# One core of Trainium2: where the context's two SSD chunks get their gate, and how often a rotary table is loaded

## The chip, the cores and the metric

The kernel runs on one core of one Trainium2 chip. The time is that of one execution on the device, in microseconds (us). Engines are called as the profile calls them: PE is TensorE's matmuls and transposes, PEld its weight loads, DVE is VectorE, ACT ScalarE, POOL GpSimd, and SP the engine whose queue issues nearly all DMAs.

## The reference, cut to what matters

The model has one even layer (a bidirectional Mamba-2 SSD group beside windowed attention) and one odd layer (S5 with GLU). The stream is 256 context tokens and 2048 latent tokens, 18 chunks or tiles of 128 tokens in all; chunks 0 and 1 are the context. The two places of the change are `ssd_output`, which every chunk passes once, and `apply_rope`, which only latent tiles pass.

```python
def ssd_output(y, xs, z, d_skip, norm_w):
    bsz, L = y.shape[:2]
    y = (y + xs * d_skip[:, None]).reshape(bsz, L, SSD_INNER)
    return rmsnorm(y * jax.nn.silu(z), norm_w)

def apply_rope(t, cos, sin):
    half = t.shape[-1] // 2
    t1, t2 = t[..., :half], t[..., half:]
    ...
    return jnp.concatenate([t1 * cos - t2 * sin, t1 * sin + t2 * cos], axis=-1)

def even_layer(x, xc, c, c_ctx, ...):
    proj = norm_mod(x, norm_w, shift, scale) @ w_in
    proj_c = norm_mod(xc, norm_w, shift_c, scale_c) @ w_in
    z, xbc, dt_raw, q, kv, g = jnp.split(proj, EVEN_SPLITS, axis=-1)
    ...
    y_c, h_f, h_b = ssd_bidir(xs_c, bm_c, cm_c, dt_c, a, h0, h0)
    y, _, _ = ssd_bidir(xs, bm, cm, dt, a, h_f, h_b)
    ssd_out = ssd_output(y, xs, z, d_skip, ssd_norm_w)
    ...
    q = apply_rope(q.reshape(bsz, L, ATT_HEADS, ATT_HEAD_DIM), cos, sin)
    k = apply_rope(k, cos, sin)
    att = window_attention(q, k, v, k_c, v_c, sink) * jax.nn.silu(g)
    x = x + gate * (jnp.concatenate([ssd_out, att], axis=-1) @ w_out)
    if ctx_out:
        ssd_c = ssd_output(y_c, xs_c, z_c, d_skip, ssd_norm_w)
        ...
```

The odd layer and the final norm come behind this and are not touched.

## The kernel before, in words

**Stages.** After some 165 us of conditioning come the input projection with the SSD sweeps (to about 1508 us in the profiled execution), attention with half of the even layer's output projection woven in (to about 2330 us), and the rest: the other half of the output projection and the odd layer.

**Matrix products.** A projection is made of three matmuls for each piece (`mm3`, lines 312 to 314: high by high, low by high, high by low parts). On PE these are the rows `mm<-xTh,wh`, `mm<-xTl,wh` and `mm<-xTh,wl` (operands the other way round in blocks that make features).

**The order of the work.** PE's order is written by hand: `even_in` makes two generators, `stream1` (the projection's blocks) and `stream2` (the SSD sweep), and `merge` (line 813) lets `stream2` have a turn whenever it has earned the PE time that a `yield` names. The other engines' orders are worked out by a scheduler from dependencies. Each engine then runs its own list strictly in order, and an instruction that waits holds all behind it on its engine; SP's DMA issues stand in such a list too.

**The backward sweep.** `stream2` first does the forward sweep, then the backward sweep `ssd_ba(c)` (line 1011) over chunks 1, 0, 17, 16, ..., 2. In `ssd_ba` PE does, for each half g, `off` (line 951) and `st` (line 928), the state's update with the tiles `xw` and `bt`. The part behind it is:

```python
        self.ssd_gt()
        if c < 2:
            nc.sync.dma_start(self.yp_d[tk, :], y)
        else:
            self.ssd_gate(c, y)
```

So the gate of chunk c is begun at the end of `ssd_ba(c)`, and its transposes (`ssd_gt`) stand one chunk later. Chunks 0 and 1 only store y there, since their z columns are projected last; their gates follow at the end of `stream2`, with y loaded back.

**The gate.** `ssd_gate` (line 1037) loads z from DRAM on SP (line 1045) and then goes from engine to engine: POOL z*y (1046), ACT Square with the row sum (1048), sixteen small DVE instructions that make 1/sqrt (1049 to 1051), ACT Copy with that scale (1052). z is a tile of tag `xw` with two buffers, which it shares with `xw`: the load of z waits until the tile that had the buffer is read for the last time. `ssd_gt` (line 1055) is eight 128x128 transposes on PE (1064) into two PSUM tiles, a DVE evacuation of each (1066) and a store (1067).

**Rotary positions.** `rope` (line 1104) is called for each of 16 latent tiles once for keys and once for queries. Each call loads a 128x128 cosine (line 1107) and a sine (1108) table of 64 KB each from DRAM, then makes two products and a sum (1111 to 1113), on DVE for the first two latent tiles (`kt < RV`, RV = 4), on POOL for the others. Around them `raw` loads the keys or queries (1117 to 1121), and `lo` (line 297) and ACT copies make the high and low parts K, KL, sA and sB that the score matmuls (1187, 1189) read. Scores go to DVE (`p`, 1200), ACT (exp, 1201), and back to PE for the transposes `pt` (1207).

Of the kernel before, what the change touches and what calls it, by code (L numbers as in the profile page):

```python
# [7 lines left out]
F32 = mybir.dt.float32  # L8
# [8 lines left out]
P = 128  # L17
# [29 lines left out]
LC, LX = 256, 2048  # L47
L = LC + LX
NT = L // P
# [206 lines left out]
class Net:  # L256
# [220 lines left out]
    def even_in(self):  # L477
        nc, i, tc = self.nc, self.i, self.tc
        with ExitStack() as st:
# [254 lines left out]
            def stream2():  # L734
                Q = []
                for c in range(NT):
                    yield ("wait", ("xbc", 0 if c < 5 else 1 if c < 11 else 2))
                    st = {}
                    for q in range(4):
                        self.ssd_fa(c, q, st)  # L740
                        Q.append((c, q, st))
                        if len(Q) > QL:
                            self.ssd_fb(*Q.pop(0))
                        yield FW
                for x in Q:
                    self.ssd_fb(*x)
                    yield FW
                for c in (1, 0) + tuple(range(17, 1, -1)):
                    if c > 1:
                        yield ("wait", ("z", c // 6))  # L750
                    for _ in self.ssd_ba(c):
                        yield 1
                yield ("wait", ("z", 0))
                for c in (1, 0):
                    self.ssd_gt()
                    self.ssd_gate(c, None)
                    yield 2
                self.ssd_gt()
            self.gz = None
            self.add(stream2(), 74 * FW + 76, 3 * (13 * 7.8 + 3 * 5 * 5.2 + 18 * 7.8) - SSD_END, (("xbc", 2), SSD_SLOW))  # L760
            self.merge(stream1())

# [306 lines left out]
    def attention(self):  # L1069

        nc, i, tc = self.nc, self.i, self.tc
        V, G, A, T = nc.vector, nc.gpsimd, nc.scalar, nc.tensor
        RING = 5
        with ExitStack() as st:
# [6 lines left out]
            qp = e(self.pool("e2q", bufs=2))  # L1081
# [13 lines left out]
            o0 = [otile()]  # L1095
            K1 = qp.tile([P, 4, (RING + 2) * P], F32R, name="K1", bufs=1)
            KL = qp.tile([P, 4, (RING + 2) * P], F32R, name="KL", bufs=1)
            VV = {}

            def slot(kt):  # L1100
                return RING + kt if kt < 2 else (kt - 2) % RING

            def rope(x, xs_, kt, n):
                t0 = (kt - 2) * P
                cs = qp.tile([P, P], F32, name="cos", bufs=2)
                sn = qp.tile([P, P], F32, name="sin", bufs=2)
                nc.sync.dma_start(cs, i["k_cos"][:, t0:t0 + P])
                nc.sync.dma_start(sn, i["k_sin"][:, t0:t0 + P])
                b = lambda t: t[:, None, :].to_broadcast([P, n, P])
                E = V if kt < RV else G  # L1110
                E.tensor_tensor(x, x, b(cs), ALU.mult)
                E.tensor_tensor(xs_, xs_, b(sn), ALU.mult)
                E.tensor_tensor(x, x, xs_, ALU.add)

            def raw(src, kt, n, tag):
                x = qp.tile([P, n, P], F32, tag=tag, name=tag)
                nc.sync.dma_start(x, dap(src, kt * P, [[L, P], [P * L, n], [1, P]]))
                if kt >= 2:
                    y = qp.tile([P, n, P], F32, tag=tag + "s", name=tag + "s")
                    for h in range(4):  # L1120
                        nc.sync.dma_start(y[h * 32:h * 32 + 32], dap(src, kt * P + (h ^ 1) * 32 * L, [[L, 32], [P * L, n], [1, P]]))
                    rope(x, y, kt, n)
                return x

            def kprep(kt):
# [15 lines left out]
                self.lo(G, vv[:, :, 64:128], v, vv[:, :, 0:64])  # L1141
                VV[kt] = vv

# [70 lines left out]
            def pvm(pv, kt, hk, hl, first, last):  # L1214

                for x, t in enumerate(hl):
                    T.matmul(pv, lhsT=VV[kt][:, hk, :], rhs=t.rearrange("p a b -> p (a b)"), start=first and x == 0, stop=last and x == 1)  # L1217

# [984 lines left out]
def consts():  # L2203
    s = np.arange(P)[:, None]
    l = np.arange(P)[None, :]
    f = np.float32
    r = np.arange(LX) // 64
    c = np.arange(LX) % 64
    inv = f(10000.0) ** (-np.arange(16, dtype=f) / f(16))
    ang = np.concatenate([r.astype(f)[:, None] * inv, c.astype(f)[:, None] * inv], axis=1).T  # L2210
    cos, sin = np.cos(ang.astype(f)), np.sin(ang.astype(f))
    band = np.concatenate([np.where(l >= s, 0, NEG), np.where(l <= s, 0, NEG)], axis=1).astype(f)
    return {"k_cos": np.concatenate([cos] * 4).astype(f), "k_sin": np.concatenate([-sin, sin] * 2).astype(f),
            "k_band": band, "k_ident": np.eye(P, dtype=f), "k_upper": (l >= s).astype(f), "k_lower": (l <= s).astype(f),
            "k_upx": (l > s).astype(f), "k_sel": (s[:NH] == np.arange(D)[None, :] // 64).astype(f)}

# [5 lines left out]
def arrays(inputs):  # L2222
    a = {}
    for k, v in inputs.items():
        v = np.ascontiguousarray(v)
        a[k] = v[0] if (k in _SQ or k[:2] in ("e_", "o_")) else v
    a.update(consts())
    return a
# [17 lines left out]
```

## Time and profile before

| what | before |
|---|---|
| runs (us) | 3739.14, 3730.95, 3734.67 |
| median (us) | 3734.67 |
| profiled execution, its time (us) | 3735.82 |
| its span (us) | 3734.0 |
| mean granted TensorE clock | 0.961 |
| PE busy | 3405.1 us, 91% of the span |
| DVE, ACT, POOL busy | 65%, 44%, 31% |
| chain that ended last | PE 28%, DVE 13%, DMA 8% of the span |
| DMA | 758.97 MB, mean 203 GB/s |

The busy shares are means over stages. The granted clock is a share of full speed: 1.00 stands for 2.4 GHz, 0.50 for 1.2 GHz. Two neighbouring PE rows overlap, since matmuls are pipelined, so the time between two starts says what one costs, not its length. The span leaves out 1.82 us of the profiled execution's time.

### The profile page before, as it was taken

What the parts mean: (1) busy time and instruction counts of PE and PEld (TensorE: products, weight loads), DVE (VectorE), ACT (ScalarE), POOL (GpSimd) and SP (SyncE); (2) the same over time, 40 slices, a digit from 0 to 9 for tenths busy, and PEclk for the clock granted to TensorE, in tenths of its full rate; (3) what the DMA queues carried; (4) which work ended last, traced back from release to release, by engine and by line L of the source; (5) the groups of instructions that cost most, each with busy time, mean ns of one, the idle gap of its engine ahead of it and who ended that gap; (6) DMA issues with size and microseconds to landing.
All of it is one profiled execution on the core that took longest, in us unless ns stands there. A gap on an engine that the chain in (4) does not pass through costs nothing.

```text
span 3734.0 us, 63256 instructions
## 1 busy us (share of the span) xinstructions
PE 3405.1 (91%) x22805; PEld 2938.9 (79%) x22805; DVE 2437.0 (65%) x5671; ACT 1652.1 (44%) x3567; POOL 1142.7 (31%) x754
## 2 busy tenths in 40 slices
PE   6879899998999998789999999988899979989999
PEld 4767788877887887668778888767688868879977
DVE  5887876565535444767677777798782699404455
ACT  4545445443422222667677775244343512343321
POOL 3221234432212332366676652210101111133121
PEclk9999999999999999899999999999899989989999
DMA  8766477875666776665545443568888844895453
GB/s 291 222 213 196 165 235 251 275 243 192 233 229 220 258 255 213 187 192 148 148 131 137 119 114 110 177 190 255 260 255 271 294 157 165 273 279 169 129 165 113
DMA packets 668004, 758.97 MB, mean 203 GB/s; under 512 B 77147, under 2 KB 529691, under 8 KB 667691
## 3 DMA queue, kind: packets, MB, share of 16 engines
q1 hardware_dynamic: 667691, 754.93, 64.3%
q8 instruction: 180, 2.95, 0.3%
q14 instruction: 133, 1.09, 0.1%
HBM read 517.62 MB, written 237.15 MB: 202 GB/s over the span
## 4 chain that ended last, share of the span: by engine, by line
PE 28%; DVE 13%; DMA 8%; SPq 2%; issue 2%; ACT 2%; POOL 1%; DVEq 0%; ACTq 0%; POOLq 0%
PE pv L1217 3%; PE pt L1207 3%; PE mm L312 2%; PE mm L313 2%; PE mm L314 2%; PE S L1187 2%; PE gpo L312 2%; PE gpo L314 2%; PE gpo L313 2%; DVE sc L1942 1%; PE S L1189 1%; DVE Bu L1947 1%; DVE sc L1945 1%; DVE sc L1943 1%; PE f L312 1%
## 5 line engine op out<-in xcount | busy, mean ns | idle before, releaser
L312 PE MATMUL mm<-xTh,wh 128*128 128x256 f32 (+2 forms) x2344 | 840.1, 358 | 71.1 <-DVE uev L1850 24.7
L313 PE MATMUL mm<-xTl,wh 128*128 128x256 f32 (+2 forms) x2344 | 783.3, 334 | 1.3 <-POOL xTl L297 0.7
L314 PE MATMUL mm<-xTh,wl 128*128 128x256 f32 (+2 forms) x2344 | 783.1, 334 | 0.8 <-DVE wl L297 0.8
L312 PEld LDWEIGHTS mm<-xTh,wh 128*128 128x128 f32 (+1 forms) x2344 | 452.3, 193 | 136.2 <-issue 48.2
L313 PEld LDWEIGHTS mm<-xTl,wh 128*128 128x128 f32 (+1 forms) x2344 | 451.8, 193 | 53.9 <-issue 14.7
L314 PEld LDWEIGHTS mm<-xTh,wl 128*128 128x128 f32 (+1 forms) x2344 | 450.3, 192 | 44.2 <-DVE wl L297 1.0
L1211 DVE TENSOR_TENSOR tl<-pt,th 128x512 fp32r<-128x512 f32 x328 | 224.3, 686 | 117.8 <-ACT th L1210 115.3
L1200 DVE TENSOR_SCALAR_CACHE_REDUCE p<-S,nsink 128x640 f32<-128x640 f32 (+2 forms) x288 | 235.3, 820 | 82.0 <-PE S L1189 79.4
L1201 ACT ACTIVATE p<-p,nm 128x640 f32<-128x640 f32 (+2 forms) x288 | 223.9, 778 | 74.7 <-DVE p L1200 72.7
L1210 ACT ACTIVATE th<-pt 128x512 fp32r<-128x512 f32 x328 | 193.8, 592 | 129.8 <-PE pt L1207 126.2
L1207 PE MATMUL pt<-ident,p 128*128 128x128 f32 x1312 | 203.6, 277 | 36.9 <-DVE tl L1211 16.7
L312 PE MATMUL mm<-wh,xTh 128*128 128x256 f32 x720 | 218.9, 304 | 18.8 <-DMA wh<-wk 9.5
L1207 PEld LDWEIGHTS pt<-ident,p 128*128 128x128 f32 x1312 | 156.8, 142 | 72.1 <-issue 22.2
L313 PE MATMUL mm<-wl,xTh 128*128 128x256 f32 x720 | 207.4, 288 | 0.7 <-DMA wl<-wk 0.7
L314 PE MATMUL mm<-wh,xTl 128*128 128x256 f32 x720 | 207.0, 288 | 0.0
L979 DVE SCALAR_TENSOR_TENSOR rf<-rb,s_P,rf 128x128 f32<-128x128 f32 x288 | 139.2, 528 | 94.2 <-ACT rf L975 90.0
L645 DVE SCALAR_TENSOR_TENSOR cA<-cR,vecs,cA 128x256 f32<-128x256 f32 (+3 forms) x192 | 179.2, 945 | 25.5 <-ACT cA L642 20.9
L424 POOL TENSOR_TENSOR xin<-xin,shr 128x1024 f32<-128x1024 f32 x33 | 86.9, 2641 | 303.1 <-DVE xin L423 298.2
L312 PEld LDWEIGHTS mm<-wh,xTh 128*128 128x128 f32 x720 | 141.7, 197 | 25.8 <-DVE zt L602 10.9
L297 POOL TENSOR_TENSOR wl<-w,wh 128x1024 fp32r<-128x1024 f32 (+1 forms) x43 | 100.3, 2335 | 187.1 <-ACT wh L305 187.0
L911 POOL TENSOR_TENSOR xw<-xs,s_de 128x1024 f32<-128x1024 f32 x36 | 72.1, 2003 | 254.4 <-DMA xs<-xs_d 169.5
L601 ACT ACTIVATE tz<-mm 128x256 f32<-128x256 f32 x144 | 53.9, 377 | 216.1 <-PE mm L314 201.7
(466 smaller groups left out, 9064.9 us busy)
## 6 DMA issues: line engine op xcount, KB each, us to landing
wh<-wk SPq DMA_DIRECT2D x116, 512.0 KB
wl<-wk SPq DMA_DIRECT2D x116, 512.0 KB
wk<-wh SPq DMA_DIRECT2D x56, 512.0 KB
wk<-wl SPq DMA_DIRECT2D x56, 512.0 KB
w<-in_e_w_in_dram SPq DMA_DIRECT2D x40, 512.0 KB
xin<-in_x_dram SPq DMA_DIRECT2D x38, 512.0 KB
rf<-prow_d SPq DMA_DIRECT2D x72, 256.0 KB
rb<-prow_d SPq DMA_DIRECT2D x72, 256.0 KB
```

The lines of the kernel that those rows point to most:

```text
L297: eng.tensor_tensor(out, x, hi.bitcast(F32), ALU.subtract)
L312: mm(ps, lhsT=ah, rhs=bh, start=first, stop=False)
L313: mm(ps, lhsT=ah, rhs=bl, start=False, stop=False)
L314: mm(ps, lhsT=al, rhs=bh, start=False, stop=last)
L645: nc.vector.scalar_tensor_tensor(acc[:, q:q + m], R[:, s + j:s + j + m], cw[:, 12 * j + b:12 * j + b + 1], acc[:, q:q + m], op0=ALU.mult, ...
L979: V.scalar_tensor_tensor(rf[:, h], rb[:, h], self.s_P[:, c, 16 + hh:17 + hh], rf[:, h], op0=ALU.add, op1=ALU.min)
L1200: V.tensor_scalar(p[:, :w], s, -0.125, nsink[:, h:h + 1], op0=ALU.mult, op1=ALU.min, accum_out=nm)
L1201: A.activation(p[:, :w], p[:, :w], AF.Exp, bias=nm, scale=-1.0, accum_out=d["sm"][:, h:h + 1])
L1207: T.transpose(pt[:, n, :], Ps[h4][:, j * P:(j + 1) * P], self.ident)
L1210: A.activation(th, pt, AF.Copy)
L1211: V.tensor_tensor(tl, pt, th.bitcast(F32), ALU.subtract)
L1217: T.matmul(pv, lhsT=VV[kt][:, hk, :], rhs=t.rearrange("p a b -> p (a b)"), start=first and x == 0, stop=last and x == 1)
```

## The change

First, the gates of context chunks 1 and 0 are no longer behind the whole sweep. They are put into it: after `ssd_ba(4)` comes the gate of chunk 1, after `ssd_ba(3)` that of chunk 0, each with a call of `ssd_gt()` ahead of it, which puts out the transposes of the chunk whose gate `ssd_ba` has just begun. The transposes' order of chunks is 5, 4, 1, 3, 0, 2 where it was 5, 4, 3, 2, 1, 0. The number of yields and their sizes are the same. Second, cosine and sine lie side by side in one table `k_cs`, 128 KB for a tile, and a tile's table is loaded once and kept in `CS` for the query's call: 16 loads of 128 KB where there were 64 of 64 KB. The pool has two buffers of the table, as it had for cosine and sine.

```diff
@@ stream2 in even_in
                     for _ in self.ssd_ba(c):
                         yield 1
-                yield ("wait", ("z", 0))
-                for c in (1, 0):
-                    self.ssd_gt()
-                    self.ssd_gate(c, None)
-                    yield 2
+                    if c in (4, 3):
+
+                        self.ssd_gt()
+                        self.ssd_gate(c - 3, None)
+                        yield 2
                 self.ssd_gt()
@@ attention
-            VV = {}
+            VV, CS = {}, {}
...
             def rope(x, xs_, kt, n):
                 t0 = (kt - 2) * P
-                cs = qp.tile([P, P], F32, name="cos", bufs=2)
-                sn = qp.tile([P, P], F32, name="sin", bufs=2)
-                nc.sync.dma_start(cs, i["k_cos"][:, t0:t0 + P])
-                nc.sync.dma_start(sn, i["k_sin"][:, t0:t0 + P])
+
+                if kt not in CS:
+                    CS[kt] = qp.tile([P, 2, P], F32, name="cs", bufs=2)
+                    nc.sync.dma_start(CS[kt], i["k_cs"][:, 2 * t0:2 * t0 + 2 * P].rearrange("p (a b) -> p a b", a=2))
+                cs, sn = CS[kt][:, 0], CS[kt][:, 1]
@@ constants
-    return {"k_cos": np.concatenate([cos] * 4).astype(f), "k_sin": np.concatenate([-sin, sin] * 2).astype(f),
+    return {"k_cs": np.stack([np.concatenate([cos] * 4).reshape(P, NT - 2, P), np.concatenate([-sin, sin] * 2).reshape(P, NT - 2, P)],
+                             axis=2).reshape(P, 2 * LX).astype(f),
```

On PE, at the transposes of chunk 5 (tile z_13723), before: the sixteen small rows of transposes are counted as x4 in each of two rows, and a projection's matmuls follow.

```order
L1064 MATMUL tp_13929<-ident_58,z_13723 128x128 x4
L1064 MATMUL tp_13937<-ident_58,z_13723 128x128 x4
L312 MATMUL mm_13982<-wh_13686,xTh_178 128x256
L313 MATMUL mm_13982<-wl_13688,xTh_178 128x256
L314 MATMUL mm_13982<-wh_13686,xTl_179 128x256
```

The same place after (z_13945 is chunk 4):

```order
L1064 MATMUL tp_13929<-ident_58,z_13723 128x128 x4
L1064 MATMUL tp_13937<-ident_58,z_13723 128x128 x4
L1064 MATMUL tp_13970<-ident_58,z_13945 128x128 x4
L1064 MATMUL tp_13978<-ident_58,z_13945 128x128 x4
L312 MATMUL mm_14013<-wh_13686,xTh_178 128x256
L313 MATMUL mm_14013<-wl_13688,xTh_178 128x256
```

The transposes of chunk 4 now stand directly behind those of chunk 5; before, some 77 rows lay between them. PE's list is the same up to here.

On PE, at the transposes of chunk 3 (z_14104) and chunk 2 (z_14284), before; left out are only more matmuls of the block:

```order
L1064 MATMUL tp_14268<-ident_58,z_14104 128x128 x4
L1064 MATMUL tp_14276<-ident_58,z_14104 128x128 x4
L312 MATMUL mm_14255<-xTh_178,wh_14158 128x512
L313 MATMUL mm_14255<-xTl_179,wh_14158 128x512
L314 MATMUL mm_14255<-xTh_178,wl_14160 128x512
...
L314 MATMUL mm_14255<-xTh_178,wl_14160 128x512
L1064 MATMUL tp_14328<-ident_58,z_14284 128x128 x4
L1064 MATMUL tp_14336<-ident_58,z_14284 128x128 x4
```

After, at the transposes of chunk 1 (z_13988), which come behind the second `st` of chunk 3 and twelve 512-wide matmuls, and of chunk 3 (z_14212):

```order
L1064 MATMUL tp_14196<-ident_58,z_13988 128x128 x4
L1064 MATMUL tp_14204<-ident_58,z_13988 128x128 x4
L312 MATMUL mm_14237<-xTh_178,wh_14067 128x256
L313 MATMUL mm_14237<-xTl_179,wh_14067 128x256
L314 MATMUL mm_14237<-xTh_178,wl_14069 128x256
...
L314 MATMUL mm_14237<-xTh_178,wl_14069 128x256
L1064 MATMUL tp_14265<-ident_58,z_14212 128x128 x4
L1064 MATMUL tp_14273<-ident_58,z_14212 128x128 x4
L312 MATMUL mm_14313<-xTh_178,wh_14152 128x512
L313 MATMUL mm_14313<-xTl_179,wh_14152 128x512
```

Between the transposes of chunk 1 and of chunk 3 stand 24 matmuls 256 wide. The last of the three places on PE is the transposes of chunk 0 (z_14283) and, 24 matmuls 512 wide later, of chunk 2 (z_14482), the last in the list:

```order
L1064 MATMUL tp_14466<-ident_58,z_14283 128x128 x4
L1064 MATMUL tp_14474<-ident_58,z_14283 128x128 x4
L312 MATMUL mm_14512<-xTh_178,wh_14386 128x512
L313 MATMUL mm_14512<-xTl_179,wh_14386 128x512
L314 MATMUL mm_14512<-xTh_178,wl_14388 128x512
...
L314 MATMUL mm_14512<-xTh_178,wl_14388 128x512
L1064 MATMUL tp_14544<-ident_58,z_14482 128x128 x4
L1064 MATMUL tp_14552<-ident_58,z_14482 128x128 x4
```

Before, 12 matmuls lay between the transposes of chunks 3 and 2, and those of chunks 1 and 0 came 48 rows and more behind them.

On DVE, at the start of attention, before: `qev` is the evacuation of the projection's last matmuls, `nsink` needs the sink's DMA, `wl0` and `wl1` are low parts of output-projection weights, `p` the first scores:

```order
L297 TENSOR_TENSOR sA_15059<-qraw_15045,sA_15059 64x1024
L1084 CAST identb_14805<-ident_58 128x128
L1088 CAST maskb_14809<-maskf_14807 128x256
L297 TENSOR_TENSOR sB_15060<-qraw_15045,sB_15060 64x1024
L602 SCALAR_TENSOR_TENSOR qev_14744<-tz_14745,mm_14719 128x256
L1092 TENSOR_SCALAR nsink_14813<-sink_14811 128x16
L602 SCALAR_TENSOR_TENSOR qev_14744<-tz_14748,mm_14719 128x256
L602 SCALAR_TENSOR_TENSOR qev_14744<-tz_14776,mm_14751 128x256
L297 TENSOR_TENSOR wl0_14963<-w3_14960,wh0_14962 128x512
L297 TENSOR_TENSOR wl1_14969<-w3_14966,wh1_14968 128x512
L1200 TENSOR_SCALAR p_14957,nm_14838<-S_14951,nsink_14813 128x512
```

After:

```order
L297 TENSOR_TENSOR sA_15045<-qraw_15035,sA_15045 64x1024
L297 TENSOR_TENSOR sB_15046<-qraw_15035,sB_15046 64x1024
L602 SCALAR_TENSOR_TENSOR qev_14744<-tz_14745,mm_14719 128x256
L1084 CAST identb_14805<-ident_58 128x128
L1088 CAST maskb_14809<-maskf_14807 128x256
L602 SCALAR_TENSOR_TENSOR qev_14744<-tz_14748,mm_14719 128x256
L602 SCALAR_TENSOR_TENSOR qev_14744<-tz_14776,mm_14751 128x256
L1092 TENSOR_SCALAR nsink_14813<-sink_14811 128x16
L1201 TENSOR_SCALAR p_14947,nm_14836<-S_14941,nsink_14813 128x512
L1201 TENSOR_SCALAR p_15014,nm_14836<-S_15008,nsink_14813 128x512
L297 TENSOR_TENSOR wl0_14953<-w3_14950,wh0_14952 128x512
```

The first two `p` now stand ahead of `wl0`, and `sA` and `sB` ahead of all three `qev`; the sink's DMA is number 993 in SP's list where it was number 1004.

## Rows read from the trace of the kernel before

**Rows 1.** Windows: stretch, us, busy us by engine, granted clock, DMA share, GB/s.

```profile
1393.00:1508.00 115.00, 97.10 (x550) 82.63 (x549) 60.97 (x161) 31.35 (x64) 26.63 (x16) 0.93 0.67 204
1508.00:2330.00 822.00, 763.02 (x5660) 635.51 (x5659) 597.55 (x1220) 573.39 (x1157) 460.47 (x286) 0.97 0.52 142
1700.00:2300.00 600.00, 582.27 (x4060) 489.64 (x4059) 438.32 (x874) 426.32 (x844) 359.28 (x219) 0.99 0.48 129
```

**Rows 2.** Waits of PE, 1380 to 1500: total us, times, longest.

```profile
PE tp L1064 <- ACT z L1052: 8.8, 1, 8.8
PE mm L312 <- issue: 8.8, 1, 8.8
```

**Rows 3.** Timeline of PE: start, length, instruction, idle before it.

```profile
1401.13 1.04 PE L1064 MATMUL tp<-ident,z 128*128 128x128 f32 x8
...
1431.37 1.02 PE L928 MATMUL st<-xw,bt 128*128 128x512 f32 x2
...
1447.61 1.97 PE L1064 MATMUL tp<-ident,z 128*128 128x128 f32 x8 [8.85 <-ACT z L1052]
...
1468.86 0.37 PE L312 MATMUL mm<-xTh,wh 128*128 128x256 f32 x1
...
1471.82 0.40 PE L312 MATMUL mm<-xTh,wh 128*128 128x512 f32 x1
...
1477.29 0.28 PE L312 MATMUL mm<-xTh,wh 128*128 128x256 f32 x1
```

**Rows 4.** Timeline, chunk 4's gate: its load and its last step.

```profile
1395.58 0.33 SPq L1045 DMA_DIRECT2D z<-z_d  x1
...
1406.63 1.15 ACT L1052 ACTIVATE z<-z,yry 128x1024 f32<-128x1024 f32 x1 [1.12 <-DVE yry L1051]
```

**Rows 5.** Timeline, chunk 2's gate: its load and its last step.

```profile
1432.59 3.80 SPq L1045 DMA_DIRECT2D z<-z_d  x2
...
1446.40 1.15 ACT L1052 ACTIVATE z<-z,yry 128x1024 f32<-128x1024 f32 x1 [1.30 <-DVE yry L1051]
```

**Rows 6.** Windows of the clock, behind a stop of PE.

```profile
1447.60:1450.70 3.10, 3.10 (x15) 3.10 (x16) 2.61 (x12) 0.00 (x0) 0.00 (x0) 0.50 0.09 28
1497.40:1502.40 5.00, 4.95 (x13) 3.94 (x14) 4.59 (x10) 2.96 (x8) 0.00 (x0) 0.54 0.79 241
```

**Rows 7.** Timeline of DVE at the start of attention.

```profile
1484.35 1.23 DVE L1111 TENSOR_TENSOR qraw<-qraw,cos 128x1024 f32<-128x1024 f32 x1 [3.09 <-DMA cos<-in_k_cos_dram]
...
1514.99 0.56 DVE L1092 TENSOR_SCALAR nsink<-sink 128x16 f32<-128x16 f32 x1 [1.09 <-DMA sink<-in_e_sink_dram]
...
1517.02 0.75 DVE L602 SCALAR_TENSOR_TENSOR qev<-tz,mm 128x256 f32<-128x256 f32 x2 [1.47 <-ACT tz L601]
1517.94 1.74 DVE L297 TENSOR_TENSOR wl<-w,wh 128x512 fp32r<-128x512 f32 x2 [0.17 <-ACT wh L1351]
1519.61 0.74 DVE L1200 TENSOR_SCALAR_CACHE_REDUCE p<-S,nsink 128x512 f32<-128x512 f32 x1
```

**Rows 8.** Timeline of PE at the start of attention.

```profile
1497.45 0.77 PE L312 MATMUL mm<-xTh,wh 128*128 128x512 f32 x1 [8.79 <-issue]
...
1520.41 0.58 PE L1187 MATMUL S<-K,sA 128*128 128x256 f32 x1 [7.00 <-DVE p L1200]
```

**Rows 9.** The cosine tables: their DMAs, and waits of their readers.

```profile
L1107 SPq DMA_DIRECT2D cos<-in_k_cos_dram x32: 328/352/1343, 1478.2 to 2100.2; - x32
...
  DMA cos<-in_k_cos_dram: 16.6, 9
```

**Rows 10.** Waits of SP's queue, 1520 to 2230: total us, times, longest.

```profile
SPq L1108 <- POOL qraws L1112: 65.8, 12, 7.4
SPq L1107 <- POOL qraw L1111: 49.3, 9, 7.0
```

**Rows 11.** Waits of PE, 1520 to 2300: the largest.

```profile
PE pt L1207 <- DVE tl L1211: 16.7, 15, 4.1
PE pt L1207 <- ACT p L1201: 13.5, 8, 4.1
```

## The prediction

> **What bounds the kernel now.** I read first the page's shares and chain: PE is busy 91% of the span, no other engine over 65%, and the chain that ended last lies on PE more than on any other engine. The change touches two stages, so I next took the windows by stage [rows 1]. In the last 115 us of the projection PE is busy 97.1; the missing 18 us are, by PE's waits, two stops of 8.8 us each [rows 2], one for the Copy of a gate, one called "issue". In attention PE has 822 − 763 = 59 us free, but from 1700 on it is busy 582 of 600. So the change is worth what it does to the few stops of PE; DVE, ACT, POOL and DMAs count only where one of them ends such a stop.
>
> The stop for the gate lies ahead of chunk 2's transposes, 8.85 us [rows 3]. The reader is to see what it is made of: from the load of z to the end of the Copy a gate takes 1407.78 − 1395.58 = 12.2 us for chunk 4 [rows 4] and 1447.55 − 1432.59 = 15.0 for chunk 2 [rows 5]. The load starts when z's buffer comes free, at the end of the chunk's second `st` (1431.37 + 1.02 = 1432.4 against 1432.59 [rows 3, 5]). A gate therefore stops PE unless 12 to 15 us of matmuls stand between a chunk's second `st` and its transposes. That is what I count.
>
> **The gates.** Nothing is removed or added on PE; the same gates and the same transposes stand in another order. By PE's list of after, three transposes stand near their gate where one did.
>
> A, ahead of chunk 4's. The list is that of before up to chunk 5's transposes, so these end where they did, at 1401.13 + 1.04 = 1402.2 [rows 3]. Chunk 4's come directly behind, and their z is ready at 1407.78 [rows 4]: a stop of 5.6. It is 4.5 if the Copy need not wait its 1.12 for DVE, 6.75 if another gate's ACT step (1.15) gets between.
>
> B, ahead of chunk 3's. From its second `st` stand twelve 512-wide matmuls, chunk 1's transposes and 24 matmuls 256 wide. 24 of 256 take 1471.82 − 1468.86 = 2.96, 24 of 512 take 1477.29 − 1471.82 = 5.47, twelve 2.74, transposes some 0.9 (their row of 1.04 less the overlap) [rows 3]. Cover 6.6 of a chain of 12.2 to 15.0: a stop of 5.6 to 8.4, taken as the middle, 7.0. Chunk 0's gate now runs at the same time, and its Square stands between chunk 3's steps on ACT and DVE; two such steps of 1.15 would make it 9.6 at most above the longer chain.
>
> C, ahead of chunk 2's. Cover 2.96 + 0.9 + 5.47 = 9.3, a stop of 2.9 to 5.7. I take 3.1, near the short chain, because no later gate is in its way.
>
> Sum 5.6 + 7.0 + 3.1 = 15.7 in place of 8.85: +6.85, bounds +4.2 and +13.2. Chunks 1 and 0 themselves come late enough: the load of chunk 1's z waits for the end of chunk 5's transposes, and 48 rows and more lie ahead of its own. That load adds a wait on SP's queue; behind it stand the stores of chunk 5 and chunk 3's y, which only DVE's sum needs, so I price it at nothing; were it not covered, it is part of B's upper end.
>
> **The clock.** After the stop of 8.85 the granted clock was 0.50 for 3.10 us, half of 2.4 GHz [rows 6], which costs 1.55. After the other it was 0.54 for 5.0, which costs 2.3. I put 1.55 on A, 1.55 on B and 0.8 on the short C, less the 1.55 of before: +2.35 (nothing to +5.4, three times 2.3 less 1.55). So the gates cost +9.2, at the ends +4.2 and +18.5.
>
> The Trainium skill ("TensorE: Matmul & The Clock Gate", Part 1: the HAM clock gate) holds the warm-up to be under 1% of a usual kernel's span and advises not to fit it. By that rule the clock term would be left out and the whole sum be 2.35 smaller. The trace agrees that it is small (1.55 of 3734), but this change's whole effect is of that size.
>
> **The start of attention.** DVE's list before has `wl0` and `wl1` ahead of the first `p`; they took 1519.61 − 1517.94 = 1.67 [rows 7], and PE waited 7.00 for `p` [rows 8]. After, both stand behind it. DVE also stood 1.09 for the sink's DMA and 1.47 for ACT's tz, together 2.56 [rows 7]; the sink's DMA now comes earlier, and sA and sB are done while tz is made. I credit 1.83 of these: −3.5 with the 1.67. Bounds: −7.0 if PE's whole stop for `p` goes; +2.5 if the last evacuation of an earlier block, which now stands behind two query products of 1.23 [rows 7] that wait for the new table, keeps its PSUM buffer from PE, which stopped 8.79 there [rows 8]. What is late next is DVE itself.
>
> **The tables.** 48 DMAs fewer at a median 352 ns on SP's queue [rows 9] are 16.9 us of issue time. Who waited for cosines sat idle 16.6 us in 9 places, all but two of them on POOL [rows 9]; SP stood 65.8 and 49.3 us behind POOL for raw tiles' buffers [rows 10], which this change leaves. PE names no table: its stops are for tl and p [rows 11]. As PE is idle 3% of the stretch from 1700 on [rows 1], I credit 3% of 16.9, −0.5. Bounds: one stop of 4.1, as long as the longest in [rows 11], more or less; more, because a table is now held from its key's call to its query's, and with two buffers the next load waits, with SP's queue behind it, for POOL's query products.
>
> The Trainium skill ("DMA: Bandwidth & Descriptors", Rules for kernel authors) says to coalesce many small transfers, those under 64 KB being mostly overhead. The loads here are of 64 KB and become 128 KB; by the rule SP's queue runs freer and the faster rival below gains. No row shows PE waiting for it.
>
> **Sum.** +9.2 − 3.5 − 0.5 = +5.2. The profiled execution took 3735.82, so 3741.0; it lies 1.15 above the median of the runs, so 3739.9 against 3734.67, given as 3740. The measurement of this kernel can tell about 0.2%, 7.5 us, from no change.
>
> **Rivals.** *Slower:* the gates cost what I say, and the start of attention returns nothing, since DVE must do the same 1.67 of `wl` and the same ropes before PE's second group of scores. Then +9.2 − 0.5 = +8.7, 3743.4 by the median, and with B at its upper end and the longer slow clock up to 3752. It decides as soon as the start returns less than 1.2 us or B exceeds 9.3. For it: DVE's first product there waits 3.09 for a table [rows 7], and what it does after that is the same work. Against: the 2.56 idle just ahead of `p`. Chance 0.32.
>
> *Faster, by the tables:* POOL's rope feeds K and sA, and what holds POOL holds the scores later. If the 16.6 us of waits for cosines [rows 9] were all on PE's path, +9.2 − 3.5 − 16.6 = −10.9, so 3723.8. For it: SP's long in-order waits [rows 10]. Against: PE's 97% [rows 1] with no wait for rope. Chance 0.12.
>
> *Faster, by the gates:* only A remains, because PE, held by A, lets the gates of chunks 3 and 2 catch up through earlier loads and free engines. Then 5.6 − 8.85 = −3.25, no more slow clock than before, −4.0 for the rest: −7.25, 3727.4. Against: the loads of z still wait for the `st` behind A, and the covers of 6.6 and 9.3 are shorter than any chain in the trace. Chance 0.06.
>
> **How the numbers follow.** My forecast has 0.50, with a range of its own of 3730 to 3750: the gates' ends −5.0 and +9.3 from my value, with part of the boundary's. The range of all cases is 3726 to 3752; it takes in the third rival and most of the slower one. Faster by over 0.2% is below 3727.2: the second rival and some of the third, 0.14. Slower is above 3742.1: most of the first rival (0.27) and the upper part of my own case (0.14), 0.41. The rest, 0.45, is within 0.2%.
>
> **What would show it.** In the trace of after, PE should have stops for the Copy of a gate ahead of three transposes, near 5.6, 7 and 3, and none ahead of chunk 1's and 0's; the clock behind the first two near 0.5. `p` should come 3 to 4 us earlier after the last projection matmul. The waits for tables should shrink without PE's busy share from 1700 on moving by more than 1%. The prediction is wrong if chunk 4's transposes don't wait, if a stop appears at chunk 1's, if B is above 10, or if attention, measured from its first score to its last, changes by more than 5 us.

## The result, and the profile after

The changed kernel takes 3779.76 us, the median of four runs (3778.76 to 3784.99), against 3734.96 before: 1.0118 times, with a 95% interval of 1.0102 to 1.0133, 44.8 us more. The forecast was 3740 and its range 3726 to 3752. The gates cost about what was forecast. The loss lies where the forecast had almost nothing: in attention.

To see where time goes I laid the two lists of PE beside each other, matmul by matmul, and took the difference of the starts (after less before). Where PE's list is the same this is a plain subtraction.

| stretch | drift at its start and end (us) | change | forecast |
|---|---|---|---|
| up to chunk 5's transposes | 0 to 9.3 | +9.3 | 0 |
| gates, to the 512-wide matmuls at 1471.8 before, 1492.0 after | 9.3 to 20.2 | +10.9 | +9.2 |
| start of attention, to the second group of scores (1520.4, 1537.3) | 20.2 to 16.9 | −3.3 | −3.5 |
| attention, to its last product (2317.5, 2361.5) | 16.9 to 44.0 | +27.1 | −0.5 |
| the rest | 44.0 to 49.2 | +5.2 | 0 |

The first and the last row are no effect that I can name. PE's list is unchanged up to chunk 5's transposes, yet in the traces of the kernels below the drift ahead of it lies between 1.5 and 9.6; and this profiled execution is the slowest of the four runs.

**The gates.** PE's timeline after, answering to [rows 3]: start, length, instruction, idle before it.

```profile
1410.44 1.04 PE L1064 MATMUL tp<-ident,z 128*128 128x128 f32 x8
1416.60 1.97 PE L1064 MATMUL tp<-ident,z 128*128 128x128 f32 x8 [5.12 <-ACT z L1052]
...
1442.96 1.03 PE L1064 MATMUL tp<-ident,z 128*128 128x128 f32 x8
1453.95 1.97 PE L1064 MATMUL tp<-ident,z 128*128 128x128 f32 x8 [7.08 <-ACT z L1052]
...
1477.63 1.03 PE L1064 MATMUL tp<-ident,z 128*128 128x128 f32 x8
1486.61 1.86 PE L1064 MATMUL tp<-ident,z 128*128 128x128 f32 x8 [2.49 <-ACT z L1052]
```

The order is 5, 4, 1, 3, 0, 2. Three stops, ahead of chunks 4, 3 and 2, of 5.12, 7.08 and 2.49, where 8.85 stood once. Behind each the eight transposes take 1.9 instead of 1.0, and the granted clock is 0.50, that is 1.2 GHz, from the end of the stop on for 5.3, 5.5 and 3.35 us (stretch, us, busy us by engine, granted clock, DMA share, GB/s):

```profile
1416.60:1421.90 5.30, 5.30 (x25) 5.30 (x26) 2.67 (x13) 1.15 (x2) 3.04 (x2) 0.50 0.67 220
1453.95:1459.45 5.50, 5.50 (x17) 4.73 (x18) 4.35 (x16) 0.42 (x1) 1.90 (x1) 0.50 0.42 131
1486.80:1490.15 3.35, 3.35 (x17) 3.35 (x17) 1.38 (x2) 0.00 (x0) 0.00 (x0) 0.50 0.24 70
```

**The start of attention.** DVE and PE after, answering to [rows 7, 8].

```profile
1535.88 0.45 DVE L1092 TENSOR_SCALAR nsink<-sink 128x16 f32<-128x16 f32 x1 [2.75 <-DMA sink<-in_e_sink_dram]
1536.46 0.75 DVE L1201 TENSOR_SCALAR_CACHE_REDUCE p<-S,nsink 128x512 f32<-128x512 f32 x1
```

```profile
1517.82 0.77 PE L312 MATMUL mm<-xTh,wh 128*128 128x512 f32 x1 [8.17 <-issue]
1532.52 0.27 PE L1194 MATMUL S<-maskb,identb 128*128 128x128 bf16 x1 [4.42 <-DVE maskb L1088]
1537.28 0.58 PE L1188 MATMUL S<-K,sA 128*128 128x256 f32 x1 [2.87 <-DVE p L1201]
```

PE waits 2.87 for `p` where it waited 7.00. For the mask it waits 4.42; before, its waits there had

```profile
PE S L1193 <- DVE maskb L1088: 3.4, 1, 3.4
```

The sink's DMA is not sooner, which I had counted on: DVE stands 2.75 for it, not 1.09. The `wl` behind `p` made up for that.

**Attention.** One window each, from the same matmul to the same matmul: before, then after (stretch, us, busy us by engine, granted clock, DMA share, GB/s).

```profile
1541.00:2317.50 776.50, 738.59 (x5482) 615.64 (x5482) 564.83 (x1159) 542.46 (x1097) 438.12 (x263) 0.99 0.50 135
```

```profile
1555.00:2361.50 806.50, 748.51 (x5484) 621.53 (x5482) 565.66 (x1163) 550.25 (x1110) 444.45 (x271) 0.97 0.48 130
```

PE does the same matmuls; of the 30 us, 20 are idle (58.0 for 37.9) and 10 are longer matmuls (748.51 for 738.59) at a lower clock. DVE's and POOL's work hardly grew. The waits say what is new. ACT's after, 1540 to 2250 (total us, times, longest):

```profile
ACT th L1211 <- PE pt L1208: 100.1, 124, 3.1
ACT p L1202 <- DVE p L1201: 63.9, 72, 2.3
ACT K L1134 <- POOL kraw L1114: 31.3, 10, 5.0
```

The third row is not there before at all. Ten times, at most of the 14 tiles whose keys POOL prepares, ACT's copy that makes K waits 3 us for POOL's key sum. What that does is one stretch of the timeline after (all engines; from 1712 to 1729):

```profile
1712.47 2.40 POOL L1113 TENSOR_TENSOR qraws<-qraws,cs 128x1024 f32<-128x1024 f32 x1 [0.38 <-DVE tl L1212]
...
1714.83 2.40 POOL L1259 TENSOR_TENSOR o<-o,gt 128x1024 f32<-128x1024 f32 x1
1714.90 0.35 SPq L1108 DMA_DIRECT2D cs<-in_k_cs_dram  x1
...
1717.17 2.41 POOL L1114 TENSOR_TENSOR qraw<-qraw,qraws 128x1024 f32<-128x1024 f32 x1
...
1719.53 0.74 POOL L1112 TENSOR_TENSOR kraw<-kraw,cs 128x256 f32<-128x256 f32 x1
1720.22 0.75 POOL L1113 TENSOR_TENSOR kraws<-kraws,cs 128x256 f32<-128x256 f32 x1
1720.91 2.40 POOL L297 TENSOR_TENSOR x3l<-x,x3h 128x1024 fp32r<-128x1024 f32 x1
1723.25 1.31 POOL L1394 TENSOR_TENSOR y<-y,xr 128x512 f32<-128x512 f32 x1
1724.50 0.75 POOL L1114 TENSOR_TENSOR kraw<-kraw,kraws 128x256 f32<-128x256 f32 x1
1725.29 0.86 ACT L1134 ACTIVATE K<-kraw 64x256 fp32r<-64x256 f32 x2 [3.02 <-POOL kraw L1114]
...
1727.25 0.60 ACT L1211 ACTIVATE th<-pt 128x512 fp32r<-128x512 f32 x1
1727.88 0.69 DVE L1212 TENSOR_TENSOR tl<-pt,th 128x512 fp32r<-128x512 f32 x1 [3.29 <-ACT th L1211]
1728.72 0.52 PE L1208 MATMUL pt<-ident,p 128*128 128x128 f32 x3 [2.66 <-DVE tl L1212]
```

Read it downward. POOL's query product ends at 1714.87; only then is a table's buffer free, and its load is issued at 1714.90. The key's products on POOL are at 1719.5, two other instructions stand between them and the sum, ACT's K copy waits 3.02 for that sum, `th` stands behind it in ACT's list, `tl` waits for `th`, and PE's transposes wait 2.66 for the PSUM buffer that `tl` reads. POOL itself works without a gap from 1712.47 to the sum, so it does not stand for the table here; the key's rows come late in its list. Then comes the slow clock, here and a tile later:

```profile
1728.70:1732.30 3.60, 3.58 (x14) 2.97 (x15) 0.55 (x1) 3.52 (x9) 3.41 (x4) 0.56 0.41 125
1778.60:1782.10 3.50, 3.47 (x12) 2.92 (x13) 0.00 (x0) 3.42 (x9) 3.31 (x4) 0.50 0.39 93
```

Before, `cos` and `sin` had two buffers each too, and calls took them in turn: key, query, key, query. So a key's table followed a key's, and a query's a query's. Now a table is loaded for the key of tile u+2 and kept for that tile's query, so each new key's load waits for the last product of an older query. The trace after has this tie at each tile: the last 12 of the 16 table loads are issued within 0.1 us of the end of the query product of two tiles before, and the key's first product follows 2.4 to 8.2 us later. It shows less as idle time of POOL, which stands for a table once in the whole trace, 1.7 us, than in the order of POOL's list: of one key tile in the middle of attention, sum and the first low part KL that needs the K copy, by their numbers in the list.

```
before  322 L1113 TENSOR_TENSOR kraw_18640<-kraw_18640,kraws_18642 128x256
        336 L297 TENSOR_TENSOR KL_14817<-kraw_18640,K1_14816 64x2x128 x2
after   333 L1114 TENSOR_TENSOR kraw_18602<-kraw_18602,kraws_18604 128x256
        334 L297 TENSOR_TENSOR KL_14817<-kraw_18602,K1_14816 64x2x128 x2
```

Fourteen rows of slack, about a tile, became one. In the rows of the traces, which leave some instructions out, the first KL stands 10 to 19 rows behind its key's sum for each of the last ten keys before, and 1 to 3 rows after.

### The profile page after: what moved, and what is told of

It reads as the page before. It is cut to its first block, busy times and chain, and to the rows that moved or that the text cites. A ratio compares the mean times of both kernels' runs of the same rounds, so it can differ in the third digit from the quotient of the medians.

```text
span 3783.2 us, 63128 instructions
## 1 busy us (share of the span) xinstructions
PE 3421.4 (90%) x22805; PEld 2948.6 (78%) x22805; DVE 2441.0 (65%) x5671; ACT 1652.7 (44%) x3567; POOL 1140.3 (30%) x754
## 5 line engine op out<-in xcount | busy, mean ns | idle before, releaser
L313 PEld LDWEIGHTS mm<-xTl,wh 128*128 128x128 f32 (+1 forms) x2344 | 452.4, 193 | 53.8 <-issue 14.7
L1218 PE MATMUL pv<-th,vv 128*128 128x512 f32 x328 | 148.8, 454 | 5.3 <-ACT sA L1150 4.6
```

The costliest lines, as they stand in the source:

```text
L313: mm(ps, lhsT=ah, rhs=bl, start=False, stop=False)
```

## The experiments

Theory H: the table held from key to query with two buffers takes the key's slack, and ACT's order hands that to PE. Rivals are named in the expectations. Beside each group the kernel before ran again on the same chip; its medians there were 3741 to 3742, so ratios are compared. "Attention" is the time from the first score matmul to the last product in the profiled execution: 809.4 before, 833.8 with the change.

**One part alone, and two cures of the table.**

```diff
 gates_only: the kernel before, and of the change only
+                    if c in (4, 3):
+                        self.ssd_gt()
+                        self.ssd_gate(c - 3, None)
+                        yield 2
 tables_only: the change, with the gates of before
 three_bufs: the change, and
-                    CS[kt] = qp.tile([P, 2, P], F32, name="cs", bufs=2)
+                    CS[kt] = qp.tile([P, 2, P], F32, name="cs", bufs=3)
-                        y = hp.tile([P, 512], F32, name="y3", bufs=2)
+                        y = hp.tile([P, 512], F32, name="y3", bufs=1)
 load_per_call: the change, and
-                if kt not in CS:
-                    CS[kt] = qp.tile([P, 2, P], F32, name="cs", bufs=2)
-                    nc.sync.dma_start(CS[kt], ...)
-                cs, sn = CS[kt][:, 0], CS[kt][:, 1]
+                ct = qp.tile([P, 2, P], F32, name="cs", bufs=2)
+                nc.sync.dma_start(ct, ...)
+                cs, sn = ct[:, 0], ct[:, 1]
```

> Only the first part of the change: the gates of chunks 1 and 0 between the sweep's last chunks; cosine and sine loaded as before. Theory H (the loss of attention comes from holding a tile's table from its key's call to its query's with two buffers): attention is as before, no ACT K copy waits for POOL, and only the three stops at the gates and the start of attention move the time: +5 to +12 us over before, 3740 to 3747. Rival S (the moved gates shift the whole schedule and attention suffers from that): 3765 or more.

> Only the second part: one table for cosine and sine, loaded once per tile, two buffers; the gates as before. Theory H: ACT's K copies wait some 30 us in all for POOL's key sum, drift over attention +22 to +32 us, time 3756 to 3767. Rival S: 3733 to 3740, attention as before.

> The whole change, but three buffers for the table (room for it: the evacuation tile y3 of the woven output projection has one buffer, not two). Theory H: the key's rope no longer waits for the query's rope of two tiles before; on POOL's list there are again some 23 rows from a key's first product to its sum, not 7; the K copies' waits fall from 31 to under 8 us, attention's drift against before to under 8, time 3738 to 3752. Rival T (it is the single 128 KB load, or the sharing itself, that is slow): stays at 3772 or above.

> The whole change, but the joint table is loaded by each call of rope, for keys and for queries (32 loads of 128 KB, the bytes of before), two buffers. Theory H: nothing is held from key to query, so attention is near before: K copies' waits under 8 us, time 3738 to 3752. Rival T (a load of 128 KB in one piece lands late, or both tables in one tile are slower to read): stays above 3765.

| kernel | ratio to before, interval | attention (us) |
|---|---|---|
| gates_only | 1.0044, 1.0031 to 1.0056 | 808.4 |
| tables_only | 1.0095, 1.0078 to 1.0112 | 836.9 |
| three_bufs | 1.0025, 1.0013 to 1.0037 | 807.3 |
| load_per_call | 1.0029, 1.0018 to 1.0040 | 805.0 |

The tables alone have the whole loss of attention, the gates none of it: rival S falls. A third buffer takes it away, and so does a load for each call; that load is of the same 128 KB, so rival T falls too. ACT's waits in tables_only:

```profile
ACT K L1134 <- POOL kraw L1114: 33.2, 10, 5.4
```

In three_bufs no such row is left; ACT's largest waits there are

```profile
ACT th L1211 <- PE pt L1208: 107.5, 132, 3.0
ACT p L1202 <- DVE p L1201: 61.3, 68, 2.1
ACT x3h L1361 <- DMA x<-ysT_d: 8.6, 2, 5.3
ACT sA L1150 <- POOL qraw L1114: 6.3, 3, 3.0
```

One sign that was expected did not come: from a key's first product to its sum POOL has 2 to 6 rows for the last ten keys, 2 to 4 in the change and 7 to 13 before. What came back is the distance from the sum to the first KL, 11 to 19 rows. The table loads still wait for query products, as before and in the change, but a tile earlier for the key that needs them: the last 11 are issued at the end of the query product of three tiles before, not two (total us, times, longest; SP's queue after, then in three_bufs):

```profile
SPq L1108 <- POOL qraws L1113: 63.5, 12, 6.9
```

```profile
SPq L1108 <- POOL qraws L1113: 61.7, 11, 7.0
```

So a long wait on a DMA queue is not by itself the loss; what counts is what stands behind it. Two times were missed. tables_only is 36 us above before by its ratio (29 to 42), where 3756 to 3767 meant 21 to 32; its attention grew by 27.5 as expected. And gates_only is 16 us above before by its ratio (11.6 to 21), more than the 12 expected at most and more than its own trace shows in the gates, the start and attention (+7.4 in all). Another 8.5 us of its drift arise behind attention, where nothing was changed.

**Was it y3, and is the gates' cost missing cover?**

```diff
 y3_one: the change, and
-                        y = hp.tile([P, 512], F32, name="y3", bufs=2)
+                        y = hp.tile([P, 512], F32, name="y3", bufs=1)
 gates_cover2: the kernel before, gates as in gates_only, but
+                        yield 2
                         self.ssd_gt()
                         self.ssd_gate(c - 3, None)
-                        yield 2
 tables_three: three_bufs with the gates of before
 both_mended: three_bufs with the gates of gates_cover2
```

> The change as it was, with one buffer of y3 alone; the table keeps two buffers. Holding as the cause: the time of the change (+38 to +50 against before), the K copies' waits still near 30 us. Rival (it was y3's single buffer that mended attention): below +20.

> The gates moved as in the change, but the two units of the projection's work stand ahead of the extra transposes and not behind the new gate (yield 2 before ssd_gt, none after); rotary tables as before. By PE's list 48 matmuls of 256 and 12 of 512 lie between the transposes of chunks 5 and 4, and 48 and 24 between those of chunks 1 and 3; between those of chunks 0 and 2 still 24 of 512. If the gates' cost is cover that is missing at the moved transposes: no stop ahead of chunk 4's and chunk 3's, 2 to 5 us ahead of chunk 2's, the stretch of the gates 6 to 10 us shorter than with the change's order and 2 to 8 shorter than before; time 10 to 18 below the gates alone. Rival (the chunk's gates there keep POOL, ACT and SP from the projection, wherever the transposes stand): the time of the gates alone, within 4 us.

> Only the tables' part, with three buffers of the table (y3 with one buffer); gates as before. Holding with too few buffers as the cause: attention within 5 us of before, whole time -6 to +4 against before, and some 35 us below the tables with two buffers. Rival (loading once per tile saves time once it is not held up): -10 or more.

> Gates with the cover ahead of the transposes, and the table with three buffers (y3 with one). If the two causes are the whole of the loss and add up: -10 to +3 us against before. Rival (something else of the change costs time): +5 or more.

| kernel | ratio to before, interval | attention (us) |
|---|---|---|
| y3_one | 1.0118, 1.0101 to 1.0135 | 833.9 |
| gates_cover2 | 0.9982, 0.9970 to 0.9993 | 805.6 |
| tables_three | 0.9991, 0.9980 to 1.0002 | 798.6 |
| both_mended | 0.9946, 0.9931 to 0.9961 | 796.9 |

y3_one is the change over again, so the cure was the third buffer. In gates_cover2, at chunks 5, 4, 1 and 2, PE's rows are

```profile
1403.35 1.04 PE L1063 MATMUL tp<-ident,z 128*128 128x128 f32 x8
1412.73 1.04 PE L1063 MATMUL tp<-ident,z 128*128 128x128 f32 x8
...
1428.16 1.03 PE L1063 MATMUL tp<-ident,z 128*128 128x128 f32 x8
...
1462.25 1.40 PE L1063 MATMUL tp<-ident,z 128*128 128x128 f32 x8 [2.79 <-ACT z L1051]
```

The stop for a gate stands now once, 2.79 us; with 60 matmuls ahead of chunk 4's transposes and 72 ahead of chunk 3's, two are gone. From chunk 5's transposes to the 512-wide matmuls of the first table this kernel takes 64.2 us, the change 81.5 and the kernel before 70.7. The kernel is 23 us below gates_only (by the ratios, 0.0062 of 3740; 10 to 18 were expected) and 7 below before: the cost was cover that was missing, not the gates' work.

tables_three agrees with no change (−3.4 by its ratio, −7.5 to +0.7), though its attention is 10.8 us shorter than before in the trace, where at most 5 were expected. With the gates of before, then, the 48 DMAs that were saved bring no gain that the measurement can tell. On moved gates the same edit does: both_mended is 13 us below gates_cover2 (0.9946 for 0.9982, with intervals that lie apart), and three_bufs 7 below gates_only (1.0025 for 1.0044, with intervals that overlap). So what loading once is worth lies between nothing and 13 us here, and the runs do not say on what it depends. both_mended is the fastest, 20 us (15 to 26) below before, where 10 at most were expected. That is more than the two parts by themselves (−6.7 and −3.4); the difference is not explained.

**By which way the loss reaches PE.**

```diff
 k_on_pool: the change, and
-                        A.activation(kh, src, AF.Copy)
+                        A.activation(kh, src, AF.Copy) if kt < KV else G.tensor_copy(kh, src)
```

> The whole change, two buffers of the table, but the copies that make K from a key of POOL's tiles run on POOL, which makes the key's sum, and no longer on ACT. POOL gets some 56 instructions more (14 tiles, four each of some 0.7 us, 40 us in all). If the loss reaches PE by way of ACT's order (a K copy waits for POOL's sum, and th, p and olo stand behind it): no wait of ACT on POOL's key sum, attention's drift over before +15 us or less, time at least 12 below the change's. Rival (the key itself is too late for the scores): PE waits at the scores for K, the drift stays at +25 or more, the time at the change's or above.

Measured: 0.9999 of before (0.9988 to 1.0010), some 45 us below the change; attention 793.2. The table is held as in the change, and the key is no earlier on POOL: for the last ten keys the sum ends 87 to 105 us before the first `p` of the tile that first reads the key, in the change 99 to 113 (before, 128 to 150). But nothing of ACT stands behind it. PE's waits for `tl` fall from 26 to

```profile
PE pt L1208 <- DVE tl L1212: 4.6, 6, 2.0
```

and no row of PE waits for K. The rival (the key too late for the scores) falls: the key was in time for PE all along. In the change's own trace the K copies of these ten keys are done 91 to 108 us before that first `p`; they only stood in ACT's list ahead of work that PE needed at once. Attention is even 16 us shorter than before. Does that come from the move alone?

```diff
 before_k: the kernel before, with k_on_pool's line
 mended_k: both_mended, with k_on_pool's line
```

> The kernel before with nothing but the K copies of POOL's tiles on POOL; tables and gates as before. If the copies cost PE time on ACT's list in the kernel before too: 8 to 18 us below before. If ACT stood for POOL's key only because the table was held: within 4 us of before, since ACT had no wait for a key sum there.

> The gates with cover ahead of the transposes, the table with three buffers, y3 with one, and the K copies of POOL's tiles on POOL. If what the copies' move gave (attention 16 us shorter than before, with the table held) comes on top of the free table: 8 to 20 us below the version without it, 25 to 38 below before. If the copies' move only cures the held table: within 4 us of the version without it.

before_k: 1.0001 (0.9991 to 1.0011), attention 802.4. mended_k: 0.9949 (0.9936 to 0.9962), the same as both_mended; attention 793.4. The move cures the held table and, in the whole time, gives nothing that can be told where none is held up. One thing does not fit: k_on_pool still has the gates' three stops (7.2 us the longest), three_bufs has such stops too, and the one is 10 us below the other. Their attention differs by 14 (793.2 and 807.3), and this stays open; the orders of POOL and ACT differ in many places between them.

## Why the prediction was wrong

**The stops: right.** 5.6, 7.0 and 3.1 were forecast, 5.12, 7.08 and 2.49 came; their sum is 14.7 for 15.7. B and C came from counting matmuls between a second `st` and its transposes, A from when chunk 4's z was ready. That A came so near has some luck in it: in the six kernels with this order of the gates it is 5.12 to 5.26 in four traces, 7.27 in load_per_call and 7.88 in y3_one. The upper end of B, 9.6, has one step of 1.15 in it, where its sentence says two (10.7); 7.08 lies below both. gates_cover2 shows that cover is what decides.

**The clock: right in kind, too small.** Three stops, three stretches at a granted clock of 0.50. They last 5.3, 5.5 and 3.35 us, which costs half of each, 7.1, less the 1.6 of before: +5.5 where +2.35 stood. The stops gave +5.8 where +6.85 stood. Together that is +11.3, near the +10.9 of the drift; that the forecast of +9.2 is so close is in part two errors against each other. By the rule weighed there (the Trainium skill, "TensorE: Matmul & The Clock Gate", Part 1) the gates would have come to +6.85, farther from the +10.9 that the trace shows.

**The start of attention: right in sum, wrong in a part.** −3.3 for −3.5. By PE's stops: 2.87 for `p` where 7.00 stood (−4.1), 4.42 for the mask where 3.40 stood (+1.0), 8.17 for 8.79 ahead of the last blocks (−0.6). The `wl` went behind `p` as said; the sink's DMA, of which I had credited some, came no sooner.

**The tables: this step failed.** The prediction priced them at −0.5, with one stop of 4.1 either way. It named the mechanism, that a table is now held from its key's call to its query's and that with two buffers the next load waits for POOL's query products. It counted this once, and saw its cost in SP's queue, which waits no longer than before (63.5 us for 65.8, twelve times each). It comes at each tile, and by way of ACT: ten waits of 3 us, 31.3 in all, and a slow clock behind the stops; +27 in the trace, and 36 us of time in tables_only. It also looked for the victim in the wrong place. "PE names no table" was read as safety [rows 11]; but the rows that PE did name, `tl` and `p`, stand on ACT's and DVE's lists, and an ACT copy that comes to wait for POOL stops all behind it. The question not asked was which instruction of ACT would newly wait, and what stands behind that one. The row of before that pointed there is SP's wait on `qraws` in [rows 10], twelve waits; after the change the twelve are waits of the loads that keys need. The prediction's own sign of being wrong, an attention changed by more than 5 us, is what came: 24.4.

**The rivals.** The slower one had the right sign, 3743 to 3752, and a wrong reason: the start of attention did return its part. The faster one, by the tables, did not come in tables_three either: with nothing held up and the gates of before, −3.4 (−7.5 to +0.7) stands where it had −16.6 for the loads; the 13 us of both_mended over gates_cover2 are nearer to it, and no run says whether they come from its reason. The faster one by the gates falls, since B and C stood, 7.08 and 2.49. The Trainium skill's rule on coalescing ("DMA: Bandwidth & Descriptors", Rules for kernel authors) names transfers under 64 KB as mostly overhead; no run here loads its tables in such pieces. From 64 to 128 KB at the same bytes no effect can be told: attention takes 805.0 in load_per_call with pieces of 128 KB, and 802.4 to 809.4 in before, gates_only, gates_cover2 and before_k with pieces of 64 KB.

**What stays open.** The sum of gates and tables in the trace (+35) is less than the 44.8 measured, and gates_only by its ratio costs 16, not the 7.4 of its own trace. The part behind attention, which no edit touches, takes 1413.8 to 1428.1 us in the thirteen traces, so a sum over one trace holds no better than some 14 us. Open are also what the table's edit is worth once its key is free, and why both mended parts together give more than their sum.

## What to carry to other kernels

When a loaded tile is kept for a second use, list for each buffer who reads it last before it is loaded anew: two buffers that used to alternate between two users were two queues, and sharing makes one of them wait for the other at every turn. Price such a wait by the number of turns, and follow it through the list of each engine that comes to wait: it costs what stands behind the waiting instruction, not what that instruction does. A gate that is moved among matmuls needs as many of them ahead of its transposes as its own chain lasts.

## What the runs showed of the hardware that was not expected

I had put POOL's copy of a key into K at 0.7 us; by the profile's median it took 0.395, about as on ACT (0.415, 64x256 f32 to fp32r). In k_on_pool, then in the change:

```profile
L1134 POOL CAST K<-kraw x56: 389/395/1388, 1528.7 to 2139.9; 64x256 fp32r<-64x256 f32 x56
```

```profile
L1134 ACT ACTIVATE K<-kraw x72: 399/415/418, 1504.2 to 2178.8; 64x256 fp32r<-64x256 f32 x72
```
